# Attention scores as 64-row matmuls: the two maps of a pair in the two halves of the array's rows

## The chip, the core and the metric

The kernel runs on one core of a Trainium2 chip. The metric is the device time of one execution in microseconds (us); the figure for a kernel is the median over its runs.

## What is computed

One layer of a decoder trunk on 256 tokens of width 1024: an RMS norm, one input projection to eight chunks of 512 columns, two kinds of attention side by side, a SiLU gate on each, and an output projection that is added to the input. With 256 tokens there is one block of keys, so the block-sparse attention (`m`, 8 heads of 64) is plain causal attention; the differential attention (`d`, 4 heads) has two softmax maps per head, each with queries and keys of 64. Cut to what matters here:

```python
mq = rms_norm(to_heads(mq), moba_q_norm)          # 8 heads of 64; mk alike
sc = einsum('bhqd,bhkd->bhqk', mq, mk) * dh**-0.5 - slope * dist     # causal
m_out = einsum('bhqk,bhkd->bhqd', softmax(sc), mv)

dq = rms_norm(dq.reshape(B, S, 4, 2, 64), diff_q_norm)     # 4 heads, 2 maps of 64; dk alike
sc = einsum('bhqcd,bhkcd->bhcqk', dq, dk) * dh**-0.5 - slope * dist  # causal
p = softmax(sc)
d_out = einsum('bhqk,bhkd->bhqd', p[:, :, 0] - lam * p[:, :, 1], dv)
x = x + concat(m_out * silu(mg), rms_norm(d_out, diff_subln) * 0.8 * silu(dg)) @ w_out
```

## The kernel before

**Numbers.** Every large matmul takes its operands as a high and a low part in float32r (`hi`, `lo`), and three passes (`PASSES`: high·high, high·low, low·high) add up in PSUM. Weights are split on the chip: ACT writes `whi` (L217), DVE writes `wlo` (L218), in pieces of 1024 columns from raw tiles `w`, which the DMA fills. There are 6 buffers of pieces; the next split waits until TensorE (PE) has used up the oldest piece, since `SPLIT_AHEAD` is 5 units.

**Order.** A unit is one k tile (128 of the 1024 inputs) of one chunk of 512 columns: 6 matmuls of 512 columns. Units 0 to 63 are the chunks `dq dk mq mk dv mv mg dg`, 8 units each; units 64 to 79 are the output projection. The table `PLAN` says before which unit each other task is issued: `("S d0", 34)` puts the scores of pair 0 of `d` before unit 34. PE executes exactly this order. The order on DVE, ACT and GpSimd (POOL) is made by a scheduler when the program is built, and each engine then goes through its list in order.

**Scores.** A pair is the two maps of a `d` head or two `m` heads; there are 8 pairs. `T_qk` transposes normed queries and keys and splits them into high and low (ACT L294, DVE L295). Queries lie with the 64 features of the pair's first map on partitions 0 to 63 and of the second on 64 to 127. Keys go into a block-diagonal tile `kbd`: for each pair there are two blocks of columns, the first map's keys with zeros below, the second's with zeros above. POOL writes the zeros once (L116, L117); each half of `kbd` has an eviction of its own. One matmul over all 128 rows so gives both maps: 512 columns for queries 128 to 255 (`s1_ps`, one PSUM bank), 256 columns for queries 0 to 127 (`s0_ps`, another). `scores` then runs, per map and query tile, one DVE instruction that adds the bias, finds the maximum and writes `p` (L319; I call these four the pair's evictions, they free its banks), and one ACT exponential with its sum (L323, the exps). For `d` DVE then forms `A`, the difference of the maps (L344, L345); for `m` it takes reciprocals `mrs` (L328).

**Banks.** PSUM has 8 banks of [128, 512], all from one pool (`bank`). Each chunk's accumulators, each pair of scores, and each pair of tiles that receives transposes (`T_banks`, and `probs_T`, the tasks `AT`) takes two. At unit 35 they are held by `acc_mq`, `acc_mk` (until `norm mqk` has written `qn`), `acc_dv` and the scores `d0`, so that the scores `d2` must take over those of `d0`. At unit 52 `acc_mg`, the sums `do_ps`, the scores `m2` and the transposes `AT d1` hold them, and `AT m0` takes over those of `AT d1`, once ACT has copied them out (`pT`, L361, L362).

Of the kernel before, what the change touches and what calls it, by code (L numbers as in the profile page):

```python
# [15 lines left out]
P = 128  # L16
# [14 lines left out]
PASSES = ((0, 0), (0, 1), (1, 0))  # L31
# segments of a pair of maps in a [128, 768] tile: (map, offset, keys); queries 128..255, then 0..127
MAPS = ((0, 0, S), (1, S, S), (0, 2 * S, P), (1, 2 * S + P, P))

# what is issued between the units of the projections (unit = one k tile of 512 columns), and when
PLAN = [
# [10 lines left out]
def kernel(  # L47
    ctx: ExitStack,
    tc: tile.TileContext,
    x: bass.AP,      # (256, 1024)  # L50
    xw: bass.AP,     # (8, 128, 768): per k tile: x transposed (256) | first 512 weight columns
    w: bass.AP,      # (18, 128, 2048): the other weights in pieces of 1 MB
    small_x: bass.AP,  # (128, 272): norm_g per k tile, mq, mk, dq, dk gains, subln | x transposed, k tile 0
    lam: bass.AP,    # (128, 256): lambda vectors
    out: bass.AP,    # (256, 1024)
):
# [15 lines left out]

# [1 line left out]
    small = const.tile([P, 16 + S], F32, name="small")  # L74
# [18 lines left out]

# [1 line left out]
    warm = const.tile([P, 1], F32, name="warm")  # L95
# [14 lines left out]
    for h in range(8):  # L110
        b = const.tile([P, S], F32, name=f"bias{h}")
        nc.gpsimd.tensor_scalar(out=b, in0=dist, scalar1=2.0 ** -(h + 1), scalar2=None, op0=ALU.mult)  # L112
        bias.append(b)
    kbd = [const.tile([P, 4, 2, S], F32R, name=f"kbd{i}") for i in range(2)]
    for t in kbd:
        nc.gpsimd.memset(t[0:64, :, 1, :].bitcast(F32), 0.0)  # L116
        nc.gpsimd.memset(t[64:128, :, 0, :].bitcast(F32), 0.0)  # L117

# [1 line left out]
    xhi = const.tile([P, KT, S], F32R, name="xhi")  # L120
# [11 lines left out]
    def rsqrt_scaled(m, n, c, f):  # L132
        """f = c / sqrt(m) for m, c [P, n] float32: a guess from the bits, a step of second order
        and one of third."""
        y = stat.tile([P, n], F32, tag="ny", name="ny")
        a = stat.tile([P, n], F32, tag="na", name="na")
        q = stat.tile([P, n], F32, tag="nq", name="nq")
        nc.vector.tensor_scalar(out=y.bitcast(I32), in0=m.bitcast(I32), scalar1=-0.5, scalar2=MAGIC,
                                op0=ALU.mult, op1=ALU.add)
        nc.vector.scalar_tensor_tensor(out=a, in0=m, scalar=-N1, in1=y, op0=ALU.mult, op1=ALU.mult)  # L140
        nc.vector.tensor_tensor(out=a, in0=a, in1=y, op=ALU.mult)
        nc.vector.scalar_tensor_tensor(out=y, in0=a, scalar=N2, in1=y, op0=ALU.add, op1=ALU.mult)
        nc.vector.scalar_tensor_tensor(out=a, in0=m, scalar=-0.5, in1=y, op0=ALU.mult, op1=ALU.mult)
        nc.vector.tensor_tensor(out=a, in0=a, in1=y, op=ALU.mult)
        if c is not None:
            nc.vector.tensor_tensor(out=y, in0=y, in1=c, op=ALU.mult)
        nc.vector.tensor_scalar(out=q, in0=a, scalar1=1.5, scalar2=2.5, op0=ALU.mult, op1=ALU.add)
        nc.vector.tensor_tensor(out=q, in0=q, in1=a, op=ALU.mult)
        nc.vector.scalar_tensor_tensor(out=f, in0=q, scalar=1.875, in1=y, op0=ALU.add, op1=ALU.mult)

# [1 line left out]
    r = const.tile([P, 2], F32, name="r")  # L152
# [17 lines left out]

# [1 line left out]
    nlam = const.tile([P, 1], F32, name="nlam")  # L172
# [11 lines left out]

# [1 line left out]
    raws, pieces = {}, {}  # L186
# [36 lines left out]
    def unit_nat(name, kt, piece):  # L223
        """x @ w, tokens on partitions: two [128, 512] accumulators."""
        if kt == 0:
            acc[name] = [bank(f"acc_{name}{t}") for t in range(2)]
        wp = pieces[piece]
        n = 256 if name == CHUNKS[0] and kt == 0 else 512
        order = [(t, i, o) for t in range(2) for i in range(3) for o in range(0, 512, n)]
        if name == CHUNKS[0]:  # L230
            order.sort(key=lambda v: (v[1], v[2]))
        for t, i, o in order:
            a, b = PASSES[i]
            c = (kt % 2) * 512 + o
            nc.tensor.matmul(acc[name][t][:, o:o + n], lhsT=(xhi, xlo)[a][:, kt, t * P:(t + 1) * P],  # L235
                             rhs=wp[b][:, c:c + n], start=kt == 0 and i == 0 and o == 0,
                             stop=kt == KT - 1 and i == 2)

# [1 line left out]
    def T_banks(nat):  # L240
# [7 lines left out]

# [1 line left out]
    nat, qk = {}, {}  # L250
# [3 lines left out]
    def squares(name):  # L254
        """sums of squares per head: [P, token tile, 8 heads of q | 8 heads of k]"""
        g, o = name[0], 8 * (name[1] == "k")
# [24 lines left out]
    def T_qk(name):  # L281
        gain = sm[:, GAIN[name]:GAIN[name] + 1]
        banks = T_banks(nat[name])
        if name[1] == "q":
            qk[name] = [work.tile([P, 4, S], F32R, tag=t, name=name) for t in ("thi", "tlo")]
            rows = [(slice(0, P), [t for t in qk[name]])]
        else:
            qk[name] = kbd
            rows = [(slice(c * 64, c * 64 + 64), [t[:, :, c] for t in kbd]) for c in range(2)]
        for t in range(2):  # L290
            ts = slice(t * P, (t + 1) * P)
            for rs, (hi, lo) in rows:
                src = banks[t][rs].rearrange("p (a b) -> p a b", a=4)
                nc.scalar.activation(out=hi[rs, :, ts], in_=src, func=AF.Copy, scale=gain[rs])  # L294
                nc.vector.scalar_tensor_tensor(out=lo[rs, :, ts], in0=src, scalar=gain[rs],  # L295
                                               in1=hi[rs, :, ts].bitcast(F32), op0=ALU.mult, op1=ALU.subtract)

# [6 lines left out]

# [1 line left out]
    probs, sums, amaps = {}, {}, {}  # L306

    def scores(g, pr):
        qt, biases = ("dq", (bias[2 * pr + 1],) * 2) if g == "d" else ("mq", (bias[2 * pr], bias[2 * pr + 1]))
        ps = [bank("s1_ps"), bank("s0_ps")]  # L310
        for o, n, qs, ks in ((0, 512, slice(P, S), slice(0, S)), (1, 256, slice(0, P), slice(0, P))):
            for i, (a, b) in enumerate(PASSES):
                nc.tensor.matmul(ps[o][:, 0:n], lhsT=qk[qt][a][:, pr, qs], rhs=kbd[b][:, pr, :, ks],  # L313
                                 start=i == 0, stop=i == 2)
        p = tile768("p")
        mx = stat.tile([P, 4], F32, tag="mx", name="nmax")
        sums[g, pr] = stat.tile([P, 4], F32, tag="sums", bufs=6, name="sums")
        for i, (c, o, n) in enumerate(MAPS):
            nc.vector.tensor_tensor_reduce(out=p[:, o:o + n], in0=ps[o // 512][:, o % 512:o % 512 + n],  # L319
                                           in1=biases[c][:, S - n:], scale=-1.0, scalar=3.0e38,  # L320
                                           op0=ALU.add, op1=ALU.min, accum_out=mx[:, i:i + 1])
        for i, (c, o, n) in enumerate(MAPS):
            nc.scalar.activation(out=p[:, o:o + n], in_=p[:, o:o + n], func=AF.Exp, scale=-1.0,  # L323
                                 bias=mx[:, i:i + 1], accum_out=sums[g, pr][:, i:i + 1])
        if g == "m":
            # 1 / sum, heads 2 pr, 2 pr + 1, queries 0..127 first
            for t in range(2):
                nc.vector.reciprocal(out=mrs[:, t, 2 * pr:2 * pr + 2], in_=sums[g, pr][:, 2 - 2 * t:4 - 2 * t])  # L328
            probs[g, pr] = [(p[:, h * S:(h + 1) * S], p[:, 512 + h * P:512 + (h + 1) * P]) for h in range(2)]
            return  # L330
        # p0 / s0 - lam * p1 / s1
        rs = stat.tile([P, 4], F32, tag="rs", name="rs")
# [17 lines left out]

# [1 line left out]
    pT = {}  # L352
# [51 lines left out]

# [1 line left out]
    mix = {}  # L406
# [28 lines left out]

# [1 line left out]
    OUT_ACC = {0: [(0, 0, 512), (1, 0, 512)], 1: [(0, 512, 512), (1, 512, 256), (1, 768, 256)]}  # L437
# [30 lines left out]

# [1 line left out]
    def task(what):  # L470
# [76 lines left out]
```

## Time and profile before

| | |
|---|---|
| time, median of 3 runs | 149.83 us (148.9 to 150.12) |
| profiled execution, first to last instruction (span) | 148.3 us |
| PE busy | 143.6 us, 97% of the span |
| DVE busy | 105.3 us, 71% |
| ACT busy | 89.1 us, 60% |
| POOL busy | 20.1 us, 14% |

The span is that of one execution and is 1.5 us shorter than the median time of the runs, which also holds what lies around it. A line of the profile names the source line (L313), the engine, and the tiles as written<-read.

### The profile page before, as it was taken

The page shows a single profiled execution, that of the slowest core. Times are in us where ns is not written, and L with a number is a line of the kernel's source. Part 1 is how long each engine was busy: PE and PEld are TensorE (multiplying, and loading weights), DVE is VectorE, ACT ScalarE, POOL GpSimd, SP SyncE. Part 2 cuts the span into 40 slices and gives each one's busy share as a digit, 9 for nine tenths or more (in the row PEclk, how much of TensorE's full clock was granted, in tenths as well). Part 3 has the DMA queues.
Part 4 walks back from the last instruction along what each step waited for, and adds up shares of the span by engine and source line. Part 5 has one row for each costly group of instructions (what it writes and reads, how often), then busy time and mean ns, then how long its engine had stood idle before and what let it go on. Part 6 is the DMA issues. An engine that isn't in the chain of part 4 may idle for free.

```text
span 148.3 us, 2108 instructions
## 1 busy us (share of the span) xinstructions
PE 143.6 (97%) x728; PEld 121.4 (82%) x728; DVE 105.3 (71%) x254; ACT 89.1 (60%) x172; POOL 20.1 (14%) x26
## 2 busy tenths in 40 slices
PE   7899999999999999999999999999999999999990
PEld 8778888888888888888988888999988888898890
DVE  2699686799899999989989997748205765730331
ACT  5467398298079666578896898757296376420000
POOL 8997000000000000000000000000056005000000
PEclk9999999999999999999999999999999999999999
DMA  3999999374980187634003662750000530000142
GB/s 99 344 407 378 422 429 367 141 285 159 362 327 7 18 309 261 261 80 203 7 0 95 205 265 44 285 241 0 2 0 0 146 141 0 0 0 0 65 152 71
DMA packets 5482, 24.39 MB, mean 164 GB/s; under 512 B 608, under 2 KB 1376, under 8 KB 3424
## 3 DMA queue, kind: packets, MB, share of 16 engines
q1 hardware_dynamic: 5472, 24.26, 45.0%
q8 instruction: 6, 0.10, 0.3%
q14 instruction: 4, 0.03, 0.1%
HBM read 23.21 MB, written 1.05 MB: 164 GB/s over the span
## 4 chain that ended last, share of the span: by engine, by line
PE 94%; DMA 2%; SPq 1%; DVE 1%; issue 0%
PE oacc L443 15%; PE acc_dq L235 9%; PE acc_dk L235 8%; PE acc_mq L235 8%; PE acc_mg L235 8%; PE acc_dg L235 8%; PE acc_mv L235 8%; PE acc_mk L235 8%; PE acc_dv L235 8%; PE s_ps L313 6%; PE T_ps L245 4%; PE mo_ps L374 2%; DMA first<-xw 2%; PE mo_ps L377 1%; PE do_ps L374 1%; PE aT_ps L357 1%
## 5 line engine op out<-in xcount | busy, mean ns | idle before, releaser
L218 DVE TENSOR_TENSOR wlo<-w,whi 128x1024 fp32r<-128x1024 f32 x36 | 43.2, 1219 | 3.8 <-ACT whi L217 3.7
L217 ACT ACTIVATE whi<-w 128x1024 fp32r<-128x1024 f32 x36 | 37.4, 1057 | 13.7 <-PE acc_dg L235 3.5
L323 ACT ACTIVATE p<-p,nmax 128x256 f32<-128x256 f32 (+1 forms) x32 | 14.1, 445 | 2.5 <-DVE nmax L319 2.5
L414 POOL TENSOR_TENSOR on<-on,mrs 128x512 f32<-128x512 f32 x2 | 2.0, 1044 | 94.3 <-ACT on L412 94.3
L449 DVE TENSOR_TENSOR o<-oacc,xn 128x512 f32<-128x512 f32 (+1 forms) x5 | 2.9, 585 | 11.1 <-PE oacc L443 11.1
L443 PE MATMUL oacc<-whi,mixm 128*128 128x512 f32 (+1 forms) x40 | 10.7, 349 | 0.0
L443 PE MATMUL oacc<-whi,mixd 128*128 128x512 f32 (+1 forms) x40 | 10.4, 347 | 0.0
L319 DVE CUSTOM_DVE_ANT_0 p<-s_ps,bias 128x256 f32<-128x256 f32 (+1 forms) x32 | 9.9, 351 | 0.4 <-PE s_ps L313 0.3
L262 DVE TENSOR_REDUCE ss<-sq 128x8 f32<-128x512 f32 x8 | 5.4, 681 | 4.0 <-ACT sq L261 4.0
L443 PEld LDWEIGHTS oacc<-whi,mixm 128*128 128x128 f32 x40 | 7.1, 188 | 1.0
L112 POOL TENSOR_SCALAR bias<-dist 128x256 f32<-128x256 f32 x8 | 7.9, 994 | 0.3
L443 PEld LDWEIGHTS oacc<-whi,mixd 128*128 128x128 f32 x40 | 7.1, 189 | 1.0
L424 DVE SCALAR_TENSOR_TENSOR on<-acc_mg,r,on 128x512 f32<-128x512 f32 x2 | 1.5, 751 | 8.3 <-POOL on L423 8.3
L235 PE MATMUL acc_dq<-whi,xhi 128*128 128x512 f32 (+1 forms) x18 | 6.5, 447 | 0.5 <-DVE whi L209 0.5
L443 PE MATMUL oacc<-wlo,mixd 128*128 128x512 f32 (+1 forms) x20 | 6.9, 347 | 0.0
L443 PE MATMUL oacc<-wlo,mixm 128*128 128x512 f32 (+1 forms) x20 | 6.9, 347 | 0.0
L235 PE MATMUL acc_mg<-whi,xhi 128*128 128x512 f32 x16 | 6.7, 421 | 0.0
L235 PE MATMUL acc_mk<-whi,xhi 128*128 128x512 f32 x16 | 6.4, 403 | 0.0
L235 PE MATMUL acc_mv<-whi,xhi 128*128 128x512 f32 x16 | 6.4, 403 | 0.0
L235 PE MATMUL acc_dg<-whi,xhi 128*128 128x512 f32 x16 | 6.4, 402 | 0.0
L235 PE MATMUL acc_mq<-whi,xlo 128*128 128x512 f32 x16 | 6.4, 397 | 0.0
L235 PE MATMUL acc_dk<-wlo,xhi 128*128 128x512 f32 x16 | 6.4, 397 | 0.0
(169 smaller groups left out, 372.7 us busy)
## 6 DMA issues: line engine op xcount, KB each, us to landing
w<-w SPq DMA_DIRECT2D x16, 1024.0 KB, 4.8
first<-xw SPq DMA_DIRECT2D x7, 384.0 KB, 5.8
w<-w SPq DMA_DIRECT2D x4, 512.0 KB, 9.1
xn<-x SPq DMA_DIRECT2D x2, 512.0 KB, 9.7
out<-o SPq DMA_DIRECT2D x3, 256.0 KB, 2.1
first<-xw SPq DMA_DIRECT2D x2, 128.0 KB, 2.6
out<-o SPq DMA_DIRECT2D x2, 128.0 KB, 1.9
small<-small_x SPq DMA_DIRECT2D x1, 136.0 KB, 2.2
```

The costliest lines, as they stand in the source:

```text
L112: nc.gpsimd.tensor_scalar(out=b, in0=dist, scalar1=2.0 ** -(h + 1), scalar2=None, op0=ALU.mult)
L217: nc.scalar.activation(out=hi, in_=sl, func=AF.Copy)
L218: nc.vector.tensor_tensor(out=lo, in0=sl, in1=hi.bitcast(F32), op=ALU.subtract)
L235: nc.tensor.matmul(acc[name][t][:, o:o + n], lhsT=(xhi, xlo)[a][:, kt, t * P:(t + 1) * P], rhs=wp[b][:, c:c + n], start=kt == 0 and i == 0 ...
L245: nc.tensor.transpose(ps[:, b * P:(b + 1) * P], nat[t][:, b * P:(b + 1) * P], ident)
L262: nc.vector.tensor_reduce(out=ssq[g][:, t, o:o + 8], in_=sq.rearrange("p (h d) -> p h d", d=64), axis=AX.X, op=ALU.add)
L313: nc.tensor.matmul(ps[o][:, 0:n], lhsT=qk[qt][a][:, pr, qs], rhs=kbd[b][:, pr, :, ks], start=i == 0, stop=i == 2)
L319: nc.vector.tensor_tensor_reduce(out=p[:, o:o + n], in0=ps[o // 512][:, o % 512:o % 512 + n], in1=biases[c][:, S - n:], scale=-1.0, scalar ...
L323: nc.scalar.activation(out=p[:, o:o + n], in_=p[:, o:o + n], func=AF.Exp, scale=-1.0, bias=mx[:, i:i + 1], accum_out=sums[g, pr][:, i:i + 1])
L374: nc.tensor.matmul(o_ps[g][t][:, c], lhsT=at[:, hh * S + t * P:hh * S + (t + 1) * P], rhs=v[:, 0, c], start=True, stop=t == 0)
L443: nc.tensor.matmul(acc["o", c][j][:, 0:n], lhsT=mix[g][a][:, kt, t * P:(t + 1) * P], rhs=pieces[piece][b][:, o:o + n], start=first and i = ...
L449: nc.vector.tensor_tensor(out=o, in0=acc["o", c][j][:, 0:n], in1=xn[:, t, col:col + n], op=ALU.add)
```

## The change

Keys are now stored like queries (`dk`, `mk` from the tags `khi`, `klo`): one eviction of all 128 partitions per token tile on ACT and DVE in place of two of 64, no zeros, no `kbd`. The scores of a pair become 12 matmuls over 64 rows each: map 0 from partitions 0 to 63, map 1 from 64 to 127, in turn, each map into its own bank, queries 128 to 255 in columns 0 to 255 and queries 0 to 127 in columns 256 to 383. The four evictions read the same numbers of elements, from other places. The rest of the diff removes comments.

```diff
-MAPS = ((0, 0, S), (1, S, S), (0, 2 * S, P), (1, 2 * S + P, P))
+MAPS = ((0, 0, S, 0), (1, S, S, 0), (0, 2 * S, P, S), (1, 2 * S + P, P, S))
...
-    kbd = [const.tile([P, 4, 2, S], F32R, name=f"kbd{i}") for i in range(2)]
-    for t in kbd:
-        nc.gpsimd.memset(t[0:64, :, 1, :].bitcast(F32), 0.0)
-        nc.gpsimd.memset(t[64:128, :, 0, :].bitcast(F32), 0.0)
...
-        if name[1] == "q":
-            qk[name] = [work.tile([P, 4, S], F32R, tag=t, name=name) for t in ("thi", "tlo")]
-            rows = [(slice(0, P), [t for t in qk[name]])]
-        else:
-            qk[name] = kbd
-            rows = [(slice(c * 64, c * 64 + 64), [t[:, :, c] for t in kbd]) for c in range(2)]
+        tags = ("thi", "tlo") if name[1] == "q" else ("khi", "klo")
+        hi, lo = qk[name] = [work.tile([P, 4, S], F32R, tag=t, name=name) for t in tags]
...
-        ps = [bank("s1_ps"), bank("s0_ps")]
-        for o, n, qs, ks in ((0, 512, slice(P, S), slice(0, S)), (1, 256, slice(0, P), slice(0, P))):
+        ps = [bank("s_ps"), bank("s_ps")]
+        for o, n, q0 in ((0, S, P), (S, P, 0)):
             for i, (a, b) in enumerate(PASSES):
-                nc.tensor.matmul(ps[o][:, 0:n], lhsT=qk[qt][a][:, pr, qs], rhs=kbd[b][:, pr, :, ks],
-                                 start=i == 0, stop=i == 2)
+                for c in range(2):
+                    rows = slice(64 * c, 64 * c + 64)
+                    nc.tensor.matmul(ps[c][:, o:o + n], lhsT=qk[g + "q"][a][rows, pr, q0:q0 + P],
+                                     rhs=qk[g + "k"][b][rows, pr, 0:n], start=i == 0, stop=i == 2)
...
-        for i, (c, o, n) in enumerate(MAPS):
-            nc.vector.tensor_tensor_reduce(out=p[:, o:o + n], in0=ps[o // 512][:, o % 512:o % 512 + n],
+        for i, (c, o, n, b) in enumerate(MAPS):
+            nc.vector.tensor_tensor_reduce(out=p[:, o:o + n], in0=ps[c][:, b:b + n],
```

The built programs show where the instructions now stand. On PE only the scores differ. Here is PE at the scores `d2` (before unit 35) with the semaphores that an instruction waits for, first before:

```order
L313 MATMUL s_ps<-kbd_133,dq 128x512 [waits DVE_49,PE_49]
L313 MATMUL s_ps<-kbd_134,dq 128x512
L313 MATMUL s_ps<-kbd_133,dq 128x512
L313 MATMUL s_ps<-kbd_133,dq 128x256 [waits DVE_49,PE_49]
L313 MATMUL s_ps<-kbd_134,dq 128x256
```

and with the change, where the two first matmuls, one for each bank, wait for DVE:

```order
L308 MATMUL s_ps<-dk,dq 128x256 [waits DVE_49] x2
L308 MATMUL s_ps<-dk,dq 128x256 x4
L308 MATMUL s_ps<-dk,dq 128x128 x6
L232 MATMUL acc_dv_600<-whi,xhi 128x512
L232 MATMUL acc_dv_600<-wlo,xhi 128x512
```

Six matmuls became twelve; a bank now holds columns of both query tiles, so it is freed by the third or fourth eviction of the pair that held it, where the first bank used to be freed by the second.

On DVE the scheduler has moved more. At the evictions of `d0` (they read `bias_119`; `w_174` and `w_176` are the raw weights 8 and 9, `w_168` and `w_170` in the changed program) the order before is

```order
L262 TENSOR_REDUCE ss<-sq 128x8 x2
L218 TENSOR_TENSOR wlo<-w_174,whi 128x1024 x2
L319 ISA p,nmax<-s_ps,bias_119 128x256
...
L319 ISA p,nmax<-s_ps,bias_119 128x128
...
L269 TENSOR_SCALAR m<-ss,r_142 128x16 x2
L218 TENSOR_TENSOR wlo<-w_176,whi 128x1024
```

and with the change

```order
L215 TENSOR_TENSOR wlo<-w_168,whi 128x1024
L135 TENSOR_SCALAR ny<-m 128x32
...
L141 TENSOR_TENSOR na<-na,ny 128x32
L215 TENSOR_TENSOR wlo<-w_170,whi 128x1024
L314 ISA p,nmax<-s_ps,bias_119 128x256
...
L314 ISA p,nmax<-s_ps,bias_119 128x128
...
L274 TENSOR_TENSOR qn<-acc_mq_391,f 128x512
```

The first split of raw weights 9 moved from behind the evictions of `d0` to ahead of them, with part of `norm mqk`; three of the four `qn` of `norm mqk` follow the evictions of `d0`, where all four used to follow those of `d1`.

On DVE at the scores of `m` (`bias_129` and `bias_131` are read by the evictions of `m3`, `bias_117` and `bias_119` by `m0`, `bias_121` by `m1`) the order before is

```order
L295 SCALAR_TENSOR_TENSOR kbd_134<-T_ps,small,kbd_133 64x4x128 x2
L218 TENSOR_TENSOR wlo<-w_180,whi 128x1024 x2
L319 ISA p,nmax<-s_ps,bias_129 128x256
...
L319 ISA p,nmax<-s_ps,bias_119 128x128
...
L319 ISA p,nmax<-s_ps,bias_121 128x256
```

and with the change

```order
L287 SCALAR_TENSOR_TENSOR mk<-T_ps,small,mk 128x4x128 x2
L215 TENSOR_TENSOR wlo<-w_174,whi 128x1024
L215 TENSOR_TENSOR wlo<-w_176,whi 128x1024 x2
L314 ISA p,nmax<-s_ps,bias_129 128x256
...
L314 ISA p,nmax<-s_ps,bias_119 128x128
...
L323 RECIPROCAL mrs<-sums 128x2 x2
L314 ISA p,nmax<-s_ps,bias_121 128x256
```

Three splits in place of two stand between the keys and the evictions of `m3`, and the reciprocals of the sums of `m0` now stand ahead of the evictions of `m1`. On ACT, the two copies `dv` (L303) stood among the exps of `d1` and after them; now they stand behind the exps of `d1` and one more split.

## Rows read from the trace of the kernel before

**Rows 1.** The page: busy time by engine, and the chain's shares by engine.

```profile
PE 143.6 (97%) x728; PEld 121.4 (82%) x728; DVE 105.3 (71%) x254; ACT 89.1 (60%) x172; POOL 20.1 (14%) x26
PE 94%; DMA 2%; SPq 1%; DVE 1%; issue 0%
```

**Rows 2.** The chain that ended last, in time: start us, us, what.

```profile
56.92 1.06 PE s_ps L313 x6
57.98 1.39 PE acc_dv L235 x6
59.37 1.05 PE s_ps L313 x6
60.42 4.20 PE acc_dv L235 x18
...
72.35 1.75 PE T_ps L245 x16
...
82.52 2.12 PE s_ps L313 x12
...
95.00 0.11 PE aT_ps L357
...
97.72 0.22 PE do_ps L377 x2
...
99.01 0.22 PE mo_ps L377 x2
```

**Rows 3.** Timeline at 74 us, PE and its weight loads: start us, us.

```profile
74.17 0.40 PE L235 MATMUL acc_mv<-wlo,xhi 128*128 128x512 f32 x1
74.17 0.19 PEld L235 LDWEIGHTS acc_mv<-whi,xlo 128*128 128x128 f32 x1
```

**Rows 4.** PE groups by form: busy us, mean ns of one.

```profile
L313 PE MATMUL s_ps<-kbd,dq 128*128 128x512 f32 x12 | 3.5, 396 | 0.0
```

**Rows 5.** Timeline of DVE: start us, us, instruction.

```profile
57.82 0.42 DVE L319 CUSTOM_DVE_ANT_0 p<-s_ps,bias 128x256 f32<-128x256 f32 x1
...
58.73 0.28 DVE L319 CUSTOM_DVE_ANT_0 p<-s_ps,bias 128x128 f32<-128x128 f32 x1
...
58.94 0.37 DVE L269 TENSOR_SCALAR m<-ss,r 128x16 f32<-128x16 f32 x2
59.22 1.22 DVE L218 TENSOR_TENSOR wlo<-w,whi 128x1024 fp32r<-128x1024 f32 x1
...
60.83 0.55 DVE L344 TENSOR_SCALAR p<-p,cf 128x256 f32<-128x256 f32 x2
...
61.95 0.42 DVE L319 CUSTOM_DVE_ANT_0 p<-s_ps,bias 128x256 f32<-128x256 f32 x1
...
67.98 1.28 DVE L277 TENSOR_TENSOR qn<-acc_mq,f 128x512 f32<-128x512 f32 x2
...
84.03 0.42 DVE L319 CUSTOM_DVE_ANT_0 p<-s_ps,bias 128x256 f32<-128x256 f32 x1
```

**Rows 6.** Timeline of ACT: start us, us, instruction, idle before and its releaser.

```profile
57.01 1.06 ACT L217 ACTIVATE whi<-w 128x1024 fp32r<-128x1024 f32 x1 [1.26 <-PE acc_dv L235]
58.29 0.51 ACT L323 ACTIVATE p<-p,nmax 128x256 f32<-128x256 f32 x1 [0.22 <-DVE nmax L319]
...
84.49 0.51 ACT L323 ACTIVATE p<-p,nmax 128x256 f32<-128x256 f32 x1 [0.24 <-DVE nmax L319]
...
89.78 0.58 ACT L361 ACTIVATE pT<-aT_ps 128x512 f32<-128x512 f32 x1
...
93.00 0.58 ACT L361 ACTIVATE pT<-aT_ps 128x512 f32<-128x512 f32 x1
```

**Rows 7.** Groups by form of DVE, ACT and POOL: busy us, mean ns of one.

```profile
L295 DVE SCALAR_TENSOR_TENSOR kbd<-T_ps,small,kbd 64x512 fp32r<-64x512 f32 x8 | 5.8, 745 | 0.5 <-ACT kbd L294 0.4
...
L294 ACT ACTIVATE kbd<-T_ps,small 64x512 fp32r<-64x512 f32 x8 | 5.2, 680 | 0.1
...
L117 POOL MEMSET kbd<- 64x1024 f32 x2 | 2.0, 976 | 0.1
```

More of the change, by code (lines that the diff above doesn't have):

```diff
@@ L283, in T_qk @@
         banks = T_banks(nat[name])
-        if name[1] == "q":
-            qk[name] = [work.tile([P, 4, S], F32R, tag=t, name=name) for t in ("thi", "tlo")]
-            rows = [(slice(0, P), [t for t in qk[name]])]
-        else:
-            qk[name] = kbd
-            rows = [(slice(c * 64, c * 64 + 64), [t[:, :, c] for t in kbd]) for c in range(2)]
+        tags = ("thi", "tlo") if name[1] == "q" else ("khi", "klo")
+        hi, lo = qk[name] = [work.tile([P, 4, S], F32R, tag=t, name=name) for t in tags]
         for t in range(2):
             ts = slice(t * P, (t + 1) * P)
[L292 to L296, printed above, removed]
+            src = banks[t].rearrange("p (a b) -> p a b", a=4)
+            nc.scalar.activation(out=hi[:, :, ts], in_=src, func=AF.Copy, scale=gain)
+            nc.vector.scalar_tensor_tensor(out=lo[:, :, ts], in0=src, scalar=gain, in1=hi[:, :, ts].bitcast(F32),
+                                           op0=ALU.mult, op1=ALU.subtract)
     vv = {}
@@ L308, in scores @@
     def scores(g, pr):
-        qt, biases = ("dq", (bias[2 * pr + 1],) * 2) if g == "d" else ("mq", (bias[2 * pr], bias[2 * pr + 1]))
-        ps = [bank("s1_ps"), bank("s0_ps")]
-        for o, n, qs, ks in ((0, 512, slice(P, S), slice(0, S)), (1, 256, slice(0, P), slice(0, P))):
+        biases = (bias[2 * pr + 1],) * 2 if g == "d" else (bias[2 * pr], bias[2 * pr + 1])
+        ps = [bank("s_ps"), bank("s_ps")]
+        for o, n, q0 in ((0, S, P), (S, P, 0)):
             for i, (a, b) in enumerate(PASSES):
-                nc.tensor.matmul(ps[o][:, 0:n], lhsT=qk[qt][a][:, pr, qs], rhs=kbd[b][:, pr, :, ks],
-                                 start=i == 0, stop=i == 2)
+                for c in range(2):
+                    rows = slice(64 * c, 64 * c + 64)
+                    nc.tensor.matmul(ps[c][:, o:o + n], lhsT=qk[g + "q"][a][rows, pr, q0:q0 + P],
+                                     rhs=qk[g + "k"][b][rows, pr, 0:n], start=i == 0, stop=i == 2)
         p = tile768("p")
@@ L317, in scores @@
         sums[g, pr] = stat.tile([P, 4], F32, tag="sums", bufs=6, name="sums")
-        for i, (c, o, n) in enumerate(MAPS):
-            nc.vector.tensor_tensor_reduce(out=p[:, o:o + n], in0=ps[o // 512][:, o % 512:o % 512 + n],
+        for i, (c, o, n, b) in enumerate(MAPS):
+            nc.vector.tensor_tensor_reduce(out=p[:, o:o + n], in0=ps[c][:, b:b + n],
                                            in1=biases[c][:, S - n:], scale=-1.0, scalar=3.0e38,
                                            op0=ALU.add, op1=ALU.min, accum_out=mx[:, i:i + 1])
-        for i, (c, o, n) in enumerate(MAPS):
+        for i, (c, o, n, _) in enumerate(MAPS):
             nc.scalar.activation(out=p[:, o:o + n], in_=p[:, o:o + n], func=AF.Exp, scale=-1.0,
```

## The prediction

> **What bounds the kernel now.** I read the page first: PE is busy for 97% of the span and the chain that ended last is PE for 94% [rows 1], so the time is PE's list of instructions plus whatever PE waits. Then the chain in order of time [rows 2]: units, scores and transposes follow each other without a gap; a unit of six 512-column matmuls takes 1.39 us, a pair of scores 1.06. Eight pairs are 8.4 us, 5.7% of the span, all of it on the path. Last I read DVE and ACT around the scores [rows 5, 6], because the order of instructions shows that the change moves work there: they have no say in the time before, and the question is by how much.
>
> **PE's part.** Before: three matmuls of 512 columns and three of 256. A 512-column one costs 1.39/6 = 0.23, so the other three cost (1.06 - 0.70)/3 = 0.12 each [rows 2]. After: six of 256 and six of 128, over 64 rows. No row shows a matmul over 64 rows, nor two at once. The nearest for the short ones: two 128-column matmuls with loads of their own (`do_ps`) take 0.22 on the chain and two of 64 columns (`mo_ps`) take 0.22 too [rows 2]. Halving the columns changes nothing, so something other than columns, in my reading the load of the weights, sets 0.11 each.
> - Lower bound, both halves side by side, loads too: 3 x 0.12 + 3 x 0.11 = 0.69 for a pair, 0.37 less than now, 3.0 us for eight.
> - Upper bound, one after the other: 6 x 0.12 + 6 x 0.11 = 1.38, 0.32 more than now, 2.6 us for eight.
>
> I take the lower: a load already runs beside the matmul ahead of it (both start at 74.17 [rows 3]), and the two halves have partitions and banks of their own. What the total owes to this choice is small below about 1.03 us for a pair, as the next part shows.
>
> The Trainium skill, "TensorE: Matmul & The Clock Gate", section "LDWEIGHTS (loading the stationary operand)", speaks against the change: a load costs by its columns, and one of fewer rows costs the same; from its figure of 128 columns at 1.2 per ns I would estimate 12 x 0.107 = 1.28 for a pair if loads come one at a time. The trace's 0.11 agrees for full loads; no run here shows one of 64 rows.
>
> **The first new wait, at the scores d2.** They take over the banks of `d0`, and so wait for the evictions of `d0`. Before, these begin at 57.82, the next instruction is at 58.94, the last ends at 59.01 [rows 5], and PE comes at 59.37: 0.36 to spare. With the change, DVE first does the `wlo` of weights 9. Its `whi` starts on ACT at 57.01, because it waits until unit 33 gives up a buffer (released by `acc_dv` [rows 6]), and ends at 58.07. The `wlo` takes 1.2, to 59.3, the evictions 1.12, to 60.4, and the banks are free at 60.5. PE can't start the scores `d2` before that: 1.1 later than now, whatever the scores cost, since PE would be there at 59.0 to 59.7.
>
> **The second, at AT m0.** From here DVE and ACT hand work to and fro, and I follow their new order with the durations of rows 5 to 7 (an estimate, each time beside the one before).
> - DVE after `d0`: four small instructions 0.4, three `qn` of 0.64, `rs` and `cf` 0.2, then `p` and `A` 1.1 (60.83 to 61.95). The evictions of `d2` start at 64.0, before 61.95.
> - ACT's exps start 0.47 after a pair's first eviction (57.82 to 58.29) and take 1.76 a pair (84.49 to 89.78 for three), so 64.5 to 66.3. Then `whi` 1.06, behind it on DVE `wlo` 1.2, `p` and `A` 1.1: the evictions of `d1` start at 69.6.
> - Exps to 71.8, `whi` to 72.9, two copies `dv` of 0.68 to 74.3. `T mk` takes over the banks of `acc_dv` and waits for these copies. `whi` to 75.3, `wlo` to 76.5: the evictions of `d3`.
> - Exps to 78.8, 0.2 and 1.1 on DVE, one `mq` and two `mk` of 0.75: 82.4. Two `wlo`: 84.8. The third waits for `whi`, behind the first copy of `mv` on ACT, behind the end of `acc_mv` on PE at 74.3 + 0.4 + 8.4 = 83.1 (from 74.10 to 82.52 it takes 8.42 [rows 2]): 84.9, so `wlo` to 86.1. There the evictions of `m3` start, before at 84.03.
> - Exps of `m3` and `m0` from 86.6 to 90.1. The evictions of `m1` now stand behind the reciprocals of the sums of `m0`, which need these exps: exps of `m1` from 90.7 to 92.4. Then one `pT`, two `whi` (before 3.2 together with a wait, from 89.78 to 93.00; 2.7 without) and the first `pT` of `d1`, 0.58: 95.9.
>
> `AT m0` takes over the bank of that `pT`; it starts at 95.00 now [rows 2], so 0.9 later. PE itself would be there at 95.00 + 1.1 - 7 x 0.37 = 93.5. So all that PE gains is waited away, and the end comes 0.9 later. If a pair stayed at 1.06, PE would come at 96.1; the two meet at a pair of about 1.03. Below that the total hardly moves. Behind `AT m0` there are no more scores, and PE runs on as before.
>
> **What is hidden.** The evictions of keys are halved: on DVE eight of 0.75 become four, 3.0 us less, and on ACT eight of 0.68, 2.7 less [rows 7]. They lie beside PE's units, and the waits above are for order, not for throughput, so I count nothing beyond the list above, where `mk` already stands with two. The zeros on POOL, four of some 0.98 [rows 7], are written long before the first scores at 56.92: nothing, and no cover is lost with them.
>
> **Sum.** 148.3 + 0.9 = 149.2 for a profiled span; the median is 1.5 above the span, so 149.83 + 0.9 = 150.7.
>
> **Rivals.**
> - **The halves come one after the other.** Then a pair costs 1.38 and PE sets the pace: 1.1 from the first wait (the first pair's extra is inside it) and 7 x 0.32 = 2.2 give 3.3, 153.1. It decides from a pair of 1.03 up. For it: the 0.11 that doesn't shrink with columns, which the change pays twelve times in place of six. Against it: separate partitions and banks.
> - **Each change between 128 and 64 rows empties the array.** A 512-column score matmul is 0.396 long in its record [rows 4] but the next starts after 0.23, so 0.16 is tail that a drained array would show, 14 times (the scores `m3` and `m0` stand together). On halves side by side a pair becomes 0.69 + 0.32 = 1.01, which the waits above hide: still 150.7. On halves in turn it is 1.70, and 1.1 + 7 x 0.64 = 5.6 make 155.4. No row shows a change of rows, for or against. The Trainium skill, "TensorEngine Tiling (Array Packing)", section "Key Properties", says that a change of tiling mode drains the engine; no run here shows it.
> - **The waits don't come.** If the scheduler's order costs nothing because DVE and ACT catch up, the lower bound for PE gives 149.83 - 3.0 = 146.8. Against it stands the wait at `d2`, which takes only three rows to work out.
>
> **How the numbers follow.** About 1%, 1.5 us, is what a measurement of this kernel can tell from no change. The forecast, side by side or nearly so with PE waiting at `d2` and at `AT m0`: 0.58; within that 149.8 to 151.8, since my list leaves out hand-overs of some 0.1 between engines and takes records for intervals elsewhere, and so mostly within 1%: 0.45, slower 0.11, faster 0.02. Halves in turn: 0.26, slower. In turn and drained: 0.08, slower. No waits: 0.06, faster. The rest, 0.02, is the same. Together faster 0.08, same 0.47, slower 0.45. The range runs from 149.4 to 153.8: it leaves out the faster case below and the drained one above, with the ends of the others.
>
> **What would show it.** In the changed profile: whether the two halves' matmuls start within some 10 ns of each other, and a pair of scores takes 0.7 or 1.4 on PE; PE idle for over 1 us ahead of the scores `d2`, released by DVE; the evictions of `d0` behind a `wlo` at about 59.3; PE idle ahead of `AT m0`, released by ACT's copies of `AT d1`; the evictions of `m3` some 2 us later than 84.03. I am wrong if PE goes through without idle time: then the handing to and fro runs faster than I add up, or PE is slower than it and the pair is the cause.

## The result and the profile after

| | before | after |
|---|---|---|
| median of 20 runs each | 149.25 us | 150.34 us |
| ratio | | 1.0083, 95% interval 1.0064 to 1.0103 |
| profiled span | 148.3 us | 148.5 us |

By the ratio the change costs 1.24 us (the medians differ by 1.09): 0.8%, clear of zero by the interval, but within the 1% that the prediction counts as no change. The forecast was 150.7, as 0.9 above a before of 149.83, which reads 149.25 here. The two spans differ by less, since in the profile of after the projections began earlier; in the other profiles of this study, too, `acc_dk` starts anywhere from 17.3 to 18.8. So I count from the start of `acc_dk`. These are the rows of the chain of waits of the kernel before that were not yet shown (start us, us, what):

```profile
18.65 11.25 PE acc_dk L235 x48
...
64.62 1.05 PE s_ps L313 x6
...
95.65 1.40 PE acc_mg L235 x6
...
98.39 0.62 PE mo_ps L374 x6
...
99.68 0.12 PE aT_ps L357
...
129.68 15.29 PE oacc L443 x87
```

The page of after, busy time by engine and the chain's shares by engine:

```profile
PE 142.6 (96%) x776; PEld 118.0 (79%) x776; DVE 102.9 (69%) x250; ACT 85.9 (58%) x168; POOL 15.8 (11%) x22
...
PE 89%; DVE 3%; DMA 3%; issue 1%; ACT 1%; SPq 1%; ACTq 0%
```

PE is still the bound, but the chain now goes through DVE once (3% here, 1% before [rows 1]). Where, the chain in time shows, for after:

```profile
17.52 11.25 PE acc_dk L232 x48
...
57.04 0.03 DVE wlo L215
57.07 1.10 issue
...
59.21 1.12 PE s_ps L308 x11
...
64.73 0.84 PE s_ps L308 x12
...
82.54 1.52 PE s_ps L308 x20
84.07 1.60 PE acc_mg L232 x6
85.66 0.84 PE s_ps L308 x9
86.50 1.59 PE acc_mg L232 x6
...
94.58 0.32 PE aT_ps L352
...
95.49 1.40 PE acc_mg L232 x6
...
98.26 0.88 PE mo_ps L369 x6
...
99.81 0.12 PE aT_ps L352
...
129.83 15.29 PE oacc L438 x87
```

(An x11, x20 or x9 in place of 12 or 24: the chain passes over some of them; the timeline has all.) Counted from `acc_dk`, with rows 2 and the rows above for before:

| place | before | after | later by |
|---|---|---|---|
| scores d2 | 40.72 | 41.69 | 0.97 |
| scores d1 | 45.97 | 47.21 | 1.24 |
| scores m3 | 63.87 | 65.02 | 1.15 |
| AT m0 | 76.35 | 77.06 | 0.71 |
| `acc_mg` behind AT m0 | 77.00 | 77.97 | 0.97 |
| AV m0 (`mo_ps`) | 79.74 | 80.74 | 1.00 |
| AT m2 behind it | 81.03 | 82.29 | 1.26 |
| end of the last `oacc` | 126.32 | 127.60 | 1.28 |

So 1.24 of it comes at one place, the scores d2: 0.97 ahead of them by the chain and the rest inside, where the row of the pair reads 1.12 and those of the other single pairs 0.84. From there to AT m0 the later pairs gain 0.53 (1.24 to 0.71), and at AT m0 and AV m0 it is lost again, 0.26 and 0.29. The timeline at d2, DVE and then PE:

```profile
57.04 1.22 DVE L215 TENSOR_TENSOR wlo<-w,whi 128x1024 fp32r<-128x1024 f32 x1
58.17 0.42 DVE L314 CUSTOM_DVE_ANT_0 p<-s_ps,bias 128x256 f32<-128x256 f32 x1
...
59.21 0.38 PE L308 MATMUL s_ps<-dk,dq 64*128 64x256 f32 x1 [0.96 <-DVE nmax L314]
```

PE stands idle for 0.96 us, released by the last evictions of d0, which stand behind the `wlo` of raw weights 9. The two small waits are in the list of who waited for whom, after (us in total, times, longest us); the kernel before has neither:

```profile
PEld mo_ps L369 <- ACT pT L356: 0.2, 1, 0.2
PEld aT_ps L352 <- ACT pT L356: 0.2, 1, 0.2
```

ACT's copies `pT` of AT d1 release AT m0, and those of AT m0 release AV m0. Next to the waits, the price of a pair: in the chain a pair now reads 0.84 where it read 1.06 [rows 2], but the unit behind it reads 1.60 or 1.59 (84.07, 86.50) where a unit took 1.40, a third of 4.20 [rows 2]. A row of the chain runs from the end of the instruction before it to its own end, so what a change of rows costs stands partly in the row behind. A pair with its unit is 0.84 + 1.59 = 2.43 at 85.66, a pair net of its unit 1.03. Two pairs with a unit are 1.52 + 1.60 = 3.12 at 82.54, net 1.72: the second pair of a group costs 0.69, and what is left, 0.34, is paid once for a trip from 128 rows to 64 and back.

### The profile page after: what moved, and what is told of

It reads as the page before. It is cut to its first block, busy times and chain, and to the rows that moved or that the text cites. A ratio compares the mean times of both kernels' runs of the same rounds, so it can differ in the third digit from the quotient of the medians.

```text
span 148.5 us, 2183 instructions
## 1 busy us (share of the span) xinstructions
PE 142.6 (96%) x776; PEld 118.0 (79%) x776; DVE 102.9 (69%) x250; ACT 85.9 (58%) x168; POOL 15.8 (11%) x22
## 4 chain that ended last, share of the span: by engine, by line
PE 89%; DVE 3%; DMA 3%; issue 1%; ACT 1%; SPq 1%; ACTq 0%
PE oacc L438 15%; PE acc_mg L232 8%; PE acc_mk L232 8%; PE acc_mq L232 8%; PE acc_dk L232 8%; PE acc_mv L232 8%; PE acc_dg L232 8%; PE acc_dq L232 7%; PE acc_dv L232 5%; PE s_ps L308 4%; PE T_ps L242 4%; DMA first<-xw 3%; PE mo_ps L369 2%; PE do_ps L369 1%; PE mo_ps L372 1%
## 5 line engine op out<-in xcount | busy, mean ns | idle before, releaser
L113 POOL TENSOR_SCALAR bias<-dist 128x256 f32<-128x256 f32 x8 | 7.3, 923 | 0.4
L232 PE MATMUL acc_dv<-whi,xhi 128*128 128x512 f32 x16 | 6.6, 415 | 0.0
L232 PE MATMUL acc_dq<-whi,xhi 128*128 128x512 f32 (+1 forms) x18 | 5.8, 406 | 0.7 <-ACT whi L208 0.5
L232 PE MATMUL acc_mg<-whi,xlo 128*128 128x512 f32 x16 | 6.3, 397 | 0.0
```

## The experiments

Theory A: the time lost is the wait at the scores d2, made by the order on DVE; on PE the halves do run side by side, but each trip to 64 rows and back costs 0.34, and so PE wins little. Rival C is the prediction's second wait in its strong form: AT m0 is held by ACT whatever the scores cost. Rival D: the 64-row scores are what is slower, and the wait only uses slack. "Length" is from the start of `acc_dk` to the end of the last `oacc`: 126.32 before, 127.60 after.

| run | ratio to before, 95% interval | length, us |
|---|---|---|
| e1, d0 one unit earlier | 1.0002 (0.9971 to 1.0033) | 126.32 |
| e2, before with the wait | 1.0067 (1.0042 to 1.0092) | 127.49 |
| e4, halves in turn | 1.0162 (1.0118 to 1.0206) | 129.00 |
| e5, fewer changes of rows | 0.9917 (0.9886 to 0.9947) | 125.67 |
| e6, two groups | 0.9912 (0.9877 to 0.9947) | 125.37 |
| e7, two passes | 0.9973 (0.9944 to 1.0001) | 126.21 |
| e8, old keys | 1.0126 (1.0082 to 1.0170) | 128.42 |
| e9, before with the plan of e5 | 0.9994 (0.9976 to 1.0013) | 126.35 |

**e1, the wait taken away from the changed kernel.**

```diff
-    ("sq mk", 33), ("S d0", 34), ("S d2", 35), ...
+    ("sq mk", 33), ("S d0", 33), ("S d2", 35), ...
```

> The changed kernel with the scores d0 issued before unit 33 in place of unit 34; DVE then evicts d0 ahead of the split of raw weights 9. Theory A (the added time is the wait at the scores d2, which comes from the order on DVE; on PE itself a pair of scores nets about 1.03 against 1.06 before): the idle time of 1 us ahead of the scores d2 is gone, the time falls by 1.0 from the changed kernel's 150.3 to 149.3, a ratio of 0.997 to 1.003 to the kernel before. Rival C (the second wait of the prediction, at AT m0, holds PE in any case): the wait moves to AT m0, the time stays at 150.0 to 150.4. Rival D (the wait only uses slack and the scores themselves are slower): 150.0 to 150.4 with no PE wait of over 0.3.

The ratio is 1.0002, the length 1.28 less than after and equal to before. The timeline, DVE and then PE:

```profile
57.63 0.42 DVE L314 CUSTOM_DVE_ANT_0 p<-s_ps,bias 128x256 f32<-128x256 f32 x1
...
59.44 0.80 PE L308 MATMUL s_ps<-dk,dq 64*128 64x256 f32 x10
```

(x10: two of the 12 start later than this window.) The evictions of d0 begin 1.8 us ahead of the scores d2, and PE goes through them without idle time. Theory A's figure, and rivals C and D both fall: nothing new took the place of the wait, and without it the change costs nothing. Nor does it gain. In the chain of e1, where `acc_dk` starts at 18.79,

```profile
94.61 0.31 PE aT_ps L352
...
99.83 0.12 PE aT_ps L352
```

AT m0 starts at 75.82, 0.53 ahead of before (76.35), and AT m2 at 81.04 (before 81.03): the two small waits, which stand in e1's list as in that of after, take all that the pairs have gained.

**e2, the wait put into the kernel before.** The split of raw weights 9 is made ready earlier, and the first eviction of d0 is ordered behind it:

```diff
+                if (g, pr, i) == ("d", 0, 0):
+                    order.enter_context(tc.issue_after(wlo[22]))
...
-        while done_s < NU // 2 and 2 * done_s <= u + SPLIT_AHEAD:
+        while done_s < NU // 2 and 2 * done_s <= u + (10 if u == 34 else SPLIT_AHEAD):
```

> The kernel before, scores unchanged, with the split of raw weights 9 put ahead of the evictions of d0 on DVE. Theory A: PE waits 0.7 to 1.1 us ahead of the scores d2 and the end comes 0.7 to 1.1 later, a ratio of 1.005 to 1.008. Rival D (what costs is the 64-row scores, not the order): the ratio stays at 0.998 to 1.002.

The ratio of 1.0067 is 1.0 us, the length 1.17 more. The chain of this kernel:

```profile
57.65 0.04 DVE wlo L218
57.68 1.22 issue
...
59.83 1.29 PE s_ps L313 x6
```

The chain shows no other wait of PE behind the first projection. With the scores untouched, the same `wlo` ahead of the same evictions makes the same loss. e1 and e2 together settle the cause: the order on DVE is enough to make the loss, and enough to undo it.

**e3, the prices by themselves.** Series of matmuls behind the kernel's work, two of them here:

```diff
+        for k in range(24):
+            nc.tensor.matmul(t[k % 2][:, 0:S], lhsT=xhi[H[k % 2], k // 2 % KT, 0:P], rhs=hi[H[k % 2], 0:S], start=True, stop=True)
...
+        for j in range(8):
+            nc.tensor.matmul(t[0], lhsT=xhi[:, j % KT, 0:P], rhs=hi[:, 0:512], start=True, stop=True)
+            nc.tensor.matmul(t[0][:, 0:S], lhsT=xhi[H[0], j % KT, 0:P], rhs=hi[H[0], 0:S], start=True, stop=True)
```

> The changed kernel with series of matmuls behind its work, whose results nobody reads: 12 of 512, 256 and 128 columns over all rows; 24 of 256 and of 128 over the two halves in turn; 12 of each over one half; eight rounds of one full 512-column matmul and one of 256 columns over one half; eight of one full one and one on each half; changes between the halves after every four. Theory A: halves in turn start two at a time, 0.12 for two of 256 columns and 0.11 or less for two of 128; one half alone 0.11 to 0.12 each; a round of full and half costs 0.234 + 0.12 plus about 0.34 for going to 64 rows and back, some 0.69, with one half or with both; changes between the halves cost nothing of the kind. Rival (the 0.34 belongs to the start of a pair of scores, its new bank and its semaphores, not to the rows): a round costs 0.35 to 0.40.

The timeline of PE, of the one execution that was taken; the price of one matmul is the distance to the next row's start, divided by the count:

```profile
145.60 2.97 PE L471 MATMUL t_ps<-whi,xhi 128*128 128x512 f32 x12
148.40 1.57 PE L473 MATMUL t_ps<-whi,xhi 128*128 128x256 f32 x12
149.81 1.45 PE L475 MATMUL t_ps<-whi,xhi 128*128 128x128 f32 x12
151.19 1.70 PE L477 MATMUL t_ps<-whi,xhi 64*128 64x256 f32 x24
152.72 1.46 PE L479 MATMUL t_ps<-whi,xhi 64*128 64x128 f32 x24
154.01 1.63 PE L481 MATMUL t_ps<-whi,xhi 64*128 64x256 f32 x12
155.48 1.45 PE L483 MATMUL t_ps<-whi,xhi 64*128 64x128 f32 x12
156.85 0.49 PE L485 MATMUL t_ps<-whi,xhi 128*128 128x512 f32 x1
...
157.59 0.50 PE L485 MATMUL t_ps<-whi,xhi 128*128 128x512 f32 x1
```

Over all rows: 0.23 for 512 columns, 0.12 for 256, 0.11 for 128. Halves in turn: 24 of 256 columns take 1.53, 24 of 128 take 1.29, so two share 0.11 to 0.13, loads included; over one half alone 12 take 1.47 and 1.37, each as much as over all rows. A round of one full matmul and one over a half takes 157.59 - 156.85 = 0.74. The parts are 0.23 + 0.12, and 0.39 is the trip, without a new bank or a semaphore: the rival falls, and the trip is a little dearer than the 0.34 expected. The later series ran at a lower clock (last section): a round takes 1.23 there, with a matmul over one half or one on each, and 32 matmuls of 256 columns that go from half to half after every four take 3.71, so 0.23 for two, less than twice the 0.13 at the full clock. A second half costs nothing more, and going between the halves shows no price. The Trainium skill, "TensorEngine Tiling (Array Packing)", section "Key Properties", says that a change of tiling mode drains the engine; this trace agrees in that a change has a price, 0.34 to 0.39 for both ways.

**e4, the halves in turn.**

```diff
+        for c in range(2):
-        for o, n, q0 in ((0, S, P), (S, P, 0)):
+            for o, n, q0 in ((0, S, P), (S, P, 0)):
...
-                for c in range(2):
```

> The changed kernel with the six matmuls of the first map issued ahead of the six of the second, the same 12 matmuls with the same banks. Theory A: the halves overlap only where neighbours in the list are of different halves, so a pair costs about 12 x 0.11 to 0.12 = 1.38 plus 0.34 for the two changes of rows, 0.7 more than now; seven pairs behind the first wait give some +4 to +5 us, 154.5 to 155.5. Rival (the engine looks far enough ahead to run the second half's list beside the first's): the time stays within 0.5 of 150.3.

The time rose by 1.2 us over after, neither of the two. The chain:

```profile
64.78 1.18 PE s_ps L308 x11
```

A pair reads 1.18, 0.34 more than interleaved, where I expected 0.7 more: PE didn't wait for the first half's list to end but started the second's beside it, part of the way. In the records of this pair the second list's first matmul starts at 65.06, the last three of the first list behind it, at 65.17, 65.23 and 65.35. The Trainium skill, "TensorE: Matmul & The Clock Gate", section "The mechanism", has PE pull a load ahead of matmuls in flight when it goes to other rows; this trace agrees (the second list's first load starts at 65.06 too). The section also has matmuls start in the program's order alone, which would make about 1.4 of this pair (12 at e3's price over one half); here the measurement decides against it. My expectation also added up seven pairs in full, though the wait at d2 and the two small waits take up part of it: AT m0 comes 1.96 later than in after, and the small waits are gone.

**e5, one trip fewer.** The plan of e1, and the scores m1 right behind m3 and m0:

```diff
-    ("T mk", 42), ("S m3", 48), ("S m0", 48), ("S m1", 49), ("AT d0", 50), ...
+    ("T mk", 42), ("S m3", 48), ("S m0", 48), ("S m1", 48), ("AT d0", 50), ...
```

> The kernel of e1 (scores d0 one unit earlier) with the scores m1 moved to stand right behind m3 and m0, so that one trip from 128 to 64 rows and back falls away; nothing else in the plan is changed. Theory A (a trip costs some 0.34 on PE, shown by the price series as 0.74 - 0.234 - 0.117 = 0.39 for a round): three pairs together take about 3 x 0.69 + 0.34 = 2.4 in place of 1.72 + 1.03 = 2.75, and the end comes 0.35 earlier than in e1, and up to 0.25 more if the wait at AV m0 goes with it: a ratio of 0.995 to 0.998 to the kernel before. Rival (the place of a pair doesn't matter, its own start costs): the ratio stays at 1.000.

The ratio is 0.9917, better than either expectation; the length is 0.65 less than e1. The chain:

```profile
81.53 2.21 PE s_ps L308 x32
83.73 3.00 PE acc_mg L232 x12
...
96.71 0.71 PE mo_ps L369 x6
```

Three pairs with two units take 5.21, net 2.41, as expected. The other 0.3 of the length are the waits at AT m0 and AV m0, which are smaller (AT m0 takes 0.76 in all, 0.90 in e1; the first row of `mo_ps` 0.71, 0.88 in e1); on ACT one `whi` moved ahead of a `pT`, so that this part isn't the trip's alone. By the runs e5 is 1.2 us faster than before, 0.8 at the near end of the interval; the trace shows 0.65 of it, and where the runs have the rest stays open.

**e6, two groups.** The scores d1 and d3 together as well:

```diff
-    ..., ("norm mqk", 37), ("S d1", 38), ("S d3", 42), ("T mq", 42),
+    ..., ("norm mqk", 37), ("S d1", 39), ("S d3", 39), ("T mq", 42),
```

> The kernel of e5 with the scores d1 and d3 put together before unit 39 as well. Theory A: one more trip less, another 0.35, so some 0.7 to 1.0 less than e1 and than the kernel before, 148.3 to 148.7, a ratio of 0.993 to 0.996. Rival: the scores d3 then come three units earlier and wait for DVE, which still holds their banks; the gain of the trip is waited away and the ratio is 0.997 to 1.000.

The chain has the two pairs as one row, without a wait ahead of it:

```profile
64.67 1.52 PE s_ps L308 x24
```

The length falls by another 0.30, about one trip. The runs, 0.9912, a little better than expected, can't tell it from e5. Both beat the kernel before by 0.8 to 0.9%, with intervals that leave out 1, and the change as it was made by some 1.7%.

**e7, a cheaper pair.** The third pass of the scores is left out:

```diff
-            for i, (a, b) in enumerate(PASSES):
+            for i, (a, b) in enumerate(PASSES[0:2]):
...
```

> The changed kernel with the third pass of the scores (low part of the queries by high part of the keys) left out, 8 matmuls a pair in place of 12, so that a pair is some 0.23 shorter. Rival C (the second wait as the prediction has it: AT m0 can't start before ACT is through with AT d1, whatever the scores cost): PE waits 1 to 1.5 at AT m0 and the time stays at 150.0 to 150.4. Theory A (behind the wait at d2 PE's own list sets the pace, the later waits are of 0.1 to 0.6): seven pairs x 0.23 = 1.6, less up to 0.5 of waits that grow: 148.7 to 149.3.

The time is 148.8, the length 1.39 less than after: against rival C as it was put. But the test isn't clean, because with fewer matmuls the scheduler put ACT's two copies `dv` in other places, in this kernel

```profile
68.00 0.69 ACT L295 ACTIVATE dv<-acc_dv,r 128x512 f32<-128x512 f32 x1 [1.00 <-PE acc_dv L232]
...
72.52 0.67 ACT L295 ACTIVATE dv<-acc_dv,r 128x512 f32<-128x512 f32 x1
```

and in after, as the prediction's list has them, in one:

```profile
71.91 1.24 ACT L295 ACTIVATE dv<-acc_dv,r 128x512 f32<-128x512 f32 x2
```

And the wait that rival C stands on is there, only earlier. The chain of e7 reaches AT m0 from ACT's copy of AT d1:

```profile
93.22 0.49 ACT pT L356
...
93.76 0.33 PE aT_ps L352
```

The timeline of e7 has PE idle for 0.23 ahead of AT m0; that of after marks no idle time there.

**e8, the old keys.** `kbd`, its zeros and its eight half evictions are kept, and the 64-row matmuls read its blocks:

```diff
-                                     rhs=qk[g + "k"][b][rows, pr, 0:n], start=i == 0, stop=i == 2)
+                                     rhs=kbd[b][rows, pr, c, 0:n], start=i == 0, stop=i == 2)
```

> The changed kernel with the keys stored as before: the block-diagonal tiles with their zeros and the eight half evictions, of which the 64-row matmuls read the blocks that hold keys. On DVE the split of raw weights 9 still stands ahead of the evictions of d0. Theory A: the wait at d2 is there as in the changed kernel (it comes with the score matmuls, not with the storage of keys), and the half evictions, 1.5 longer on DVE at each of two places, may add up to 0.6 at the scores m3, whose keys come late: 150.3 to 151.0. Rival (the storage of keys is what moved the order or cost time): 149.2 to 149.5, as before.

The time is 151.18, just above what was expected, the length 0.82 more than after. The wait at d2 is there as well, so the rival falls: what moved the order on DVE is the score matmuls, not the keys. The rest comes at the scores m3 and m0, in the timeline of PE:

```profile
83.19 0.50 PE L317 MATMUL s_ps<-kbd,mq 64*128 64x256 f32 x3
84.00 1.49 PE L317 MATMUL s_ps<-kbd,mq 64*128 64x256 f32 x21 [0.31 <-DVE kbd L296]
```

The scores m3 wait for the last half evictions of the keys; the two pairs take 2.22 to the next unit at 85.41 where after takes 1.52.

**e9, the control.** The kernel before with both moves of e5's plan:

```diff
-    ("sq mk", 33), ("S d0", 34), ("S d2", 35), ...
-    ("T mk", 42), ("S m3", 48), ("S m0", 48), ("S m1", 49), ...
+    ("sq mk", 33), ("S d0", 33), ("S d2", 35), ...
+    ("T mk", 42), ("S m3", 48), ("S m0", 48), ("S m1", 48), ...
```

> The kernel before, with its scores over all 128 rows, and the two moves of the plan of e5: scores d0 one unit earlier, m1 right behind m3 and m0. Theory A (what e5 gains is trips between 128 and 64 rows, of which this kernel has none): nothing to gain, a ratio of 0.998 to 1.002. Rival (the moves help by themselves, as better places for the evictions): a ratio of 0.991 to 0.996, as e5.

The ratio is 0.9994. So the moves as such are worth nothing; in e5 they pay with the scores that make trips.

## Why the prediction was right, and where not

- **The wait at the scores d2** came as worked out: forecast 1.1 later, measured 0.97 ahead of the scores by the chain and 1.24 with the wait inside them (the first matmuls of the two maps start at 59.21 and 59.42 there, elsewhere together; each waits for a bank of its own). On the clock of before (after + 1.13, the difference of the two `acc_dk`) the evictions of d0 begin at 59.30, forecast 59.3, and PE at 60.34, forecast 60.5.
- **The pair.** Halves side by side, loads too, at 0.69 is what the second pair of a group costs (1.72 - 1.03), and the sign that was named holds: at d1 the two first matmuls start at 64.661 and 64.664. What the forecast's case left out is the trip, 0.34 each time. This is the second rival's figure with halves side by side: 0.69 + 0.32 = 1.01, measured 1.03. So the step that failed is "I take the lower", 0.69 for every pair; of the 3.0 us that this gave PE, six single pairs at 1.03 and two together at 1.72 leave 8.48 - 7.90 = 0.6. The time came out right all the same, because 1.03 is where the prediction had PE and the chain through DVE and ACT meet. That the pair lies just there is luck. The prediction's estimate of 1.28 for a pair takes the Trainium skill's price of a load ("TensorE: Matmul & The Clock Gate", section "LDWEIGHTS (loading the stationary operand)") for loads that come one at a time. That is not what the two halves do: two loads and two matmuls share 0.11 to 0.13 in e3.
- **The second wait.** The list of hand-overs held, but for a slip: its last step adds up to 92.4 + 2.7 + 0.58 = 95.7, not 95.9, so that the list gives 0.7 for the end and not 0.9. On the clock of before, the copies `dv` end at 74.28 (forecast 74.3) and AT m0 starts at 95.71 (forecast 95.9); the evictions of m3 and the first `pT` of d1, in two rows of after, DVE and ACT,

```profile
84.88 0.42 DVE L314 CUSTOM_DVE_ANT_0 p<-s_ps,bias 128x256 f32<-128x256 f32 x1
...
93.92 0.59 ACT L356 ACTIVATE pT<-aT_ps 128x512 f32<-128x512 f32 x1
```

begin at 86.01 (forecast 86.1) and end at 95.64 (95.7 by the list's terms). What the timeline of after doesn't mark is the idle time of PE ahead of AT m0 that was to show it: PE came 0.7 later itself, and lost 0.26 at AT m0 (0.71 later ahead of it, 0.97 behind), where the sum had PE waiting 2.4 (from 93.5 to 95.9).
- **"All that PE gains is waited away"** holds for the 0.53 that there was to gain, in after and in e1, though half of it went at AV m0. For a pair well below 1.03 it stays open. e7's cheaper pair took 1.4 off, against it, but on another order of ACT, on which ACT's copies of AT d1 came 1.4 earlier too and PE waited for them; with after's order held no cheaper pair was run.
- **"Behind `AT m0` ... PE runs on as before"** was wrong by 0.29 (0.97 to 1.26): AV m0 waits for the `pT` of m0. With it the term of 0.9 for the end is 1.28 in the trace and 1.24 by the runs.
- **What is hidden.** Nothing for the keys was right for the sum, since the list already had them with two evictions. e8 gives their worth: with the half evictions the change would have cost 0.8 more.
- **The rivals.** Halves in turn, 153.1: not so as the change issues them, and only 1.2 above after where e4 forces them apart. No waits, 146.8: without the wait at d2 e1 is at 149.47, because seven trips take 2.4 of PE's 3.0 and the two small waits the rest. Each change of rows empties the array, 150.7 with halves side by side: this is the one that came, as far as the price goes.

## What to carry to other kernels

When a scheduler orders some engines, a change on one engine is first a change of order on the others: look which wait for a buffer comes to stand in front of what the bound engine needs next, and try a move of one table entry before giving up the change. Matmuls over half the rows pay in groups: a pair of lists in the two halves costs what one list costs, but going there and back costs as much as three matmuls of 256 columns, so put all such work side by side and count the trips, not only the matmuls. The price of such a trip stands partly in the row of the next instruction, so compare sums over both.

## What the runs showed of the hardware

- PE starts the second half's list beside the first's although it stands behind it in the program (e4: 1.18 a pair, where 12 in a row at e3's 0.11 to 0.12 would take 1.4). So "PE executes exactly this order", in the section on the kernel before, does not hold for starts in two halves.
- Over one half the matmuls of e3 cost as much as over all 128 rows, 0.12 for 256 columns and 0.11 for 128: fewer rows alone save nothing.
- In e3's rounds the granted clock fell. Windows of that kernel: from:to, us, PE busy, PEld busy, DVE, ACT, POOL, granted clock, DMA share, GB/s:

```profile
156.80:159.00 2.20, 2.20 (x8) 1.11 (x6) 0.00 (x0) 0.00 (x0) 0.00 (x0) 1.00 0.00 0
...
160.50:165.00 4.50, 4.50 (x8) 2.00 (x7) 0.00 (x0) 0.00 (x0) 0.00 (x0) 0.50 0.00 0
```

From 156.8 the engine did nothing but rounds of one full matmul and one over a half. From about 159 on it was granted 0.50, 1.2 GHz, and a round took 1.23 in place of 0.74. Ahead of the rounds, from 151.2, stood matmuls over halves alone, at 1.00; no run here separates what brought the clock down. The seven trips that the change spreads over the kernel leave it at 0.998 for the whole span, and e1's seven at 1.000.
